# Modulation vectors of two transformer blocks: multiplying two row chunks of weights in one step instead of one

## The chip, the cores and the metric

The kernel runs on one core of a Trainium2 chip. The metric is the device time of one execution in microseconds (us); lower is better. Everything below concerns that one core, its engines and its DMA queues: PE (the matrix engine), DVE, ACT, POOL and SP, the last of which issues nearly all transfers.

## What is computed

Two blocks stand one behind the other in the same launch. The first takes 512 tokens of width 1024 through four layers (gated linear attention, a spatial gating unit, forgetting attention, gated linear attention again). The second takes them through two layers with a feed-forward part each; its first layer mixes a gated delta rule with latent attention, its second neighbourhood attention with grouped attention, and both also see 256 context tokens. Each layer is modulated by vectors that depend on the condition alone:

```python
def first_block(x, c, ...):
    cond = jax.nn.silu(c)
    for i in range(DEPTH):
        mod = (cond @ w_mod[i] + b_mod[i])[:, None, :]
        shift, scale, gate = jnp.split(mod, 3, axis=-1)
        h = rms_norm(x, norm_pre_g[i]) * (1.0 + scale) + shift
        ...
        x = x + gate * rms_norm(o, norm_post_g[i])
```

The second block does the same with six vectors for each layer and two conditions (one for the tokens, one for the context). So there are 4 x 3 + 2 x 6 = 24 vectors of 1024 numbers, each a product of a condition with a 1024 x 1024 matrix of fp32 weights, that is 4 MB to be read for each vector. The change touches only how 22 of them are made; the first two are made in a setup that it leaves alone.

## The kernel before, in words

The program is written as Python generators. A main generator walks through the layers; each of its yields marks a small piece of work (some tens of PE instructions). Two queues of background generators run beside it: "m" makes the modulation vectors and, near the end of it, a table of neighbourhood biases in DRAM (`nab`); "c" does the context tokens. `drain` (L416) steps each queue by a rate per yield of the main generator: 0.6 steps of queue "m" (`MRATE`). `step` (L399) adds up what is owed and takes whole steps. In the last column chunk of an output projection `proj_tok` also takes `MB` = 2 steps of queue "m" behind each row tile (L316 to L322). `need` (L411) takes steps until a vector that is wanted now is finished.

One vector is one run of `mods` (L373). Its weights go in eight row chunks of 128 x 1024 fp32 (512 KB). A chunk is loaded by SP (L382) into a tile of tag `wm`, of which there are two buffers (`WM` = 2), and multiplied by four matmuls of PE (L386). These stand in four column groups of one PSUM bank (tile `mods.pa`, 32 columns of the condition's padded tile as stationary and 256 moving columns each); an fp32 matmul is two passes, so a chunk is eight instructions on PE. The generator yields after each chunk: a step loads chunk k and multiplies chunk k - 1. After the last, DVE copies the bank to SBUF (L390) and SP stores the vector to a scratch tensor in DRAM (L392). That is eleven steps for a vector. `mod_cols` (L425) later loads two vectors of the scratch and their bias (tiles `mra`, `mrb`), DVE adds them (L432), and PE turns the sum into columns. `na_bias` (L1931) writes the table `nab` by 4 stores of a constant (L1940), 15 transfers for the border columns (L1947) and 8 for the inner ones (L1952), with yields between.

The generators set only the order in which the program is written. A scheduler then places each instruction on its engine by estimated readiness, so that chunks of one vector can be drawn together or apart. Within an engine the order is then fixed; an instruction that waits holds up all behind it. All loads are issued by SP, in turn: weight pieces of the projections (L279, tiles that end in `wr`, which ACT and POOL split into `wh` and `wl`), chunks `wm`, and small loads. Products of the main work read `wh` and `wl`: L307 to L309 for tokens as stationary or moving side, L351 to L353 for the others; the part of a tile's name ahead of the dot is the stage (`out` output projection, `sgu` gating unit, `gdng` delta rule, `mlap` latent attention's projections, `pre` norms).

Of the kernel before, what the change touches and what calls it, by code (L numbers as in the profile page):

```python
# [10 lines left out]
F32 = mybir.dt.float32  # L11
# [10 lines left out]
D = 1024  # L22
# [26 lines left out]
class Residual:  # L49
# [8 lines left out]
    def load(self):  # L58
        nc = self.core.nc
        self.tiles = [self.core.t("t4", (128, D)) for _ in range(self.nt)]  # L60
        for i, tl in enumerate(self.tiles):
            nc.sync.dma_start(tl, self.src[i * 128:(i + 1) * 128])
# [14 lines left out]
class Core:  # L77
# [295 lines left out]
    def mods(self, scr, cname, W, ncond, v):  # L373

        nc = self.nc
        pad = self.cond[cname]
        ps = self.psA()
        ws = []
        for k in range(8 + WM - 1):
            if k < 8:  # L380
                ws.append(self.wp.tile([128, D], F32, name=self.nm("wm"), tag="wm", bufs=WM))
                nc.sync.dma_start(ws[k], W[k * 128:(k + 1) * 128, v * D:(v + 1) * D])  # L382
            j = k - WM + 1
            if j >= 0:
                for g in range(4):
                    nc.tensor.matmul(ps[g * 32:(g + 1) * 32, :256], pad[:, j, :], ws[j][:, g * 256:(g + 1) * 256],  # L386
                                     start=(j == 0), stop=(j == 7))
            yield
        sb = self.t("t1", [128, 256])
        nc.vector.tensor_copy(sb, ps[:, :256])  # L390
        for i in range(ncond):
            nc.sync.dma_start(scr[i, v * D:(v + 1) * D].rearrange("(g n) -> g n", n=256), sb[i:128:32, :])  # L392
        yield
# [1656 lines left out]
    def ffn_layer(self, H, x, nt, mods, ic, i, nxt, dst=None):  # L2050
        A = self.A
        self.need(("b", i, 3))
        gg = self.gate_row(mods, ic, A["b_mod_2"][i], 5, A["g_post_ffn_2"][i])
        return (yield from self.phase("ffn", self.ffn(H, nt, i, x, gg, nxt, dst)))
# [59 lines left out]
    def even_out(self, x, nt, mods, ic, s, nxt):  # L2114
        A = self.A
        self.need(("b", 0, 1))
        gg = self.gate_row(mods, ic, A["b_mod_2"][0], 2, A["g_post_mix_2"][0])
        ffn = lambda: self.norm_before(x, nt, mods, ic, "ffn", 0)
        H = yield from self.phase("out", self.outproj(s["O"], nt, A["w_out_even_2"][0], 8, x, gg, ffn))
        if nt == 4:  # L2120
            self.context_rate(12)
        return (yield from self.ffn_layer(H, x, nt, mods, ic, 0, nxt))
# [76 lines left out]
WM, WSZ = 2, 512  # L2199
# [9 lines left out]
BANKS, ROLES = {"pp": 4, "pa": 4}, {}  # L2209
LO = {'': 'p', 'pre': 'ppd', 'c': 'ddp', 'cgdnp': 'd', 'cmlap': 'd', 'gla': 'ppd', 'oddq': 'pdd', 'coddkv': 'pd', 'gdnp': 'ppd', 'oddkv': 'pdd', 'out': 'ddp', 'cout': 'pd', 'mlap': 'ppd', 'fox': 'pdd', 'cmla': 'd'}  # L2210
PREA = (3,)
MRATE, MB = 0.6, 2
ADV = 1
PRI = 100
LEAD = (1, 1, 1, 1, 2)
# [66 lines left out]
```

## Time and profile before

| | us |
|---|---|
| runs | 3272.90, 3277.65, 3279.38 |
| median | 3277.65 |
| profiled execution, its own time | 3278.63 |
| its span, first to last instruction | 3276.8 |
| its mean granted PE clock | 0.975 |

The profiled execution lies 1.8 us outside its span and 1.0 us above the median of the runs. Busy times in the profile are sums over instructions; a matmul's end is modelled and overlaps the start of the next, so the cost of one in a chain is read from the starts of its neighbours. A wait in brackets, such as [1.62 <-DMA mods.wm<-in_w_mod_dram], is time in which the engine had nothing to run, and what ended it. A granted clock of 1.00 is 2.4 GHz, of 0.50 it is 1.2 GHz.

### The profile page before, as it was taken

How to read it: one execution, taken by the hardware profiler on the slowest of the kernel's cores; microseconds unless marked ns; L12 is line 12 of the kernel's file. 1: busy time of each engine (PE TensorE's matmuls, PEld its weight loads, DVE VectorE, ACT ScalarE, POOL GpSimd, SP SyncE). 2: the span in 40 equal slices, each digit the busy share in tenths (PEclk: the TensorE clock that was granted, in tenths of full speed). 3: DMA queues.
4: the chain of work that ended last, by engine and by line, in shares of the span. 5: the costliest groups of instructions: out<-in, count | busy, mean ns of one | idle time of the engine just before them, and what ended most of it. 6: DMA issues, size and time to landing. Idle time of an engine off the chain costs nothing.

```text
span 3276.8 us, 63046 instructions
## 1 busy us (share of the span) xinstructions
PE 3100.1 (95%) x24399; PEld 2687.7 (82%) x24399; DVE 1691.3 (52%) x3578; ACT 1460.2 (45%) x3205; POOL 1308.6 (40%) x1320
## 2 busy tenths in 40 slices
PE   6999999999999999988989999899999989999998
PEld 4878889778877778777877889899899867889898
DVE  2745564454555564666888667641113468641212
ACT  3434544454544533345545544453324457643323
POOL 2544454232212345344543123554445341254445
PEclk7999999999999999989999999899999999999999
DMA  7355645753436524444564334443333330143332
GB/s 238 91 157 168 210 139 162 246 162 118 135 120 186 184 80 136 129 140 141 166 164 133 102 94 138 140 136 94 97 120 111 109 84 2 41 131 96 96 121 87
DMA packets 487155, 426.36 MB, mean 130 GB/s; under 512 B 108038, under 2 KB 441065, under 8 KB 486857
## 3 DMA queue, kind: packets, MB, share of 16 engines
q1 hardware_dynamic: 486857, 422.35, 43.0%
q8 instruction: 192, 3.15, 0.4%
q14 instruction: 106, 0.87, 0.1%
HBM read 383.66 MB, written 38.03 MB: 129 GB/s over the span
## 4 chain that ended last, share of the span: by engine, by line
PE 74%; DVE 11%; DMA 5%; ACT 4%; issue 3%; POOL 2%; SPq 1%; DVEq 0%; POOLq 0%; ACTq 0%
PE ffn.pp L352 6%; PE ffn.pp L351 6%; PE ffn.pp L353 6%; PE ffn.pp L308 3%; PE ffn.pp L307 3%; PE ffn.pp L309 3%; PE mods.pa L386 3%; PE out.pp L307 2%; PE out.pp L309 2%; PE out.pp L308 2%; DMA mods.wm<-in_w_mod_dram 2%; PE fox.pp L308 1%; PE fox.pp L309 1%; PE fox.pp L307 1%; PE sgu.pp L307 1%
## 5 line engine op out<-in xcount | busy, mean ns | idle before, releaser
L257 POOL TENSOR_TENSOR ffn.wl<-ffn.wr,ffn.wh 128x512 fp32r<-128x512 f32 x258 | 333.6, 1294 | 355.2 <-ACT ffn.wh L256 355.2
L256 ACT ACTIVATE ffn.wh<-ffn.wr 128x512 fp32r<-128x512 f32 x258 | 162.5, 631 | 355.2 <-PE ffn.pp L353 144.3
L351 PE MATMUL ffn.pp<-pre.t,ffn.wh 128*128 128x512 f32 x672 | 261.5, 389 | 0.0
L352 PE MATMUL ffn.pp<-pre.t,ffn.wl 128*128 128x512 f32 x672 | 261.5, 389 | 0.0
L353 PE MATMUL ffn.pp<-pre.t,ffn.wh 128*128 128x512 f32 x672 | 261.4, 389 | 0.0
L308 PE MATMUL ffn.pp<-ffn.wl,ffn.t 128*128 128x256 f32 x656 | 185.3, 283 | 0.0
L309 PE MATMUL ffn.pp<-ffn.wh,ffn.t 128*128 128x256 f32 x656 | 184.9, 283 | 0.0
L307 PE MATMUL ffn.pp<-ffn.wh,ffn.t 128*128 128x256 f32 x656 | 184.7, 283 | 0.0
L591 DVE SCALAR_TENSOR_TENSOR ffn.t<-ffn.t,ffn.pp 128x512 f32<-128x512 f32 (+1 forms) x66 | 39.4, 597 | 252.1 <-ACT ffn.t L590 252.0
L257 POOL TENSOR_TENSOR gla.wl<-gla.wr,gla.wh 128x512 fp32r<-128x512 f32 x66 | 87.0, 1319 | 163.2 <-ACT gla.wh L256 153.6
L307 PE MATMUL gla.pp<-gla.wh,pre.t 128*128 128x256 f32 x512 | 150.0, 293 | 0.7 <-ACT gla.t L644 0.4
L309 PE MATMUL gla.pp<-gla.wh,pre.t 128*128 128x256 f32 x512 | 149.1, 292 | 0.9 <-DVE pre.t L257 0.9
L308 PE MATMUL gla.pp<-gla.wl,pre.t 128*128 128x256 f32 x512 | 149.1, 291 | 0.0
L353 PEld LDWEIGHTS ffn.pp<-pre.t,ffn.wh 128*128 128x128 f32 x672 | 126.1, 188 | 26.2
L351 PEld LDWEIGHTS ffn.pp<-pre.t,ffn.wh 128*128 128x128 f32 x672 | 126.2, 188 | 26.1
L352 PEld LDWEIGHTS ffn.pp<-pre.t,ffn.wl 128*128 128x128 f32 x672 | 126.2, 188 | 25.9
L257 POOL TENSOR_TENSOR ffn.cwl<-ffn.cwr,ffn.cwh 128x512 fp32r<-128x512 f32 x44 | 60.8, 1382 | 211.9 <-ACT ffn.cwh L256 172.7
L386 PE MATMUL mods.pa<-mods.wm,cond_c 128*32 128x256 f32 x1408 | 122.5, 403 | 16.0 <-DMA mods.wm<-in_w_mod_dram 15.9
L1133 DVE SCALAR_TENSOR_TENSOR ffn.t<-ffn.t,ffn.pp 128x512 f32<-128x512 f32 (+1 forms) x66 | 39.4, 597 | 176.3 <-PE ffn.pp L353 175.7
L256 ACT ACTIVATE ffn.cwh<-ffn.cwr 128x512 fp32r<-128x512 f32 x132 | 82.9, 632 | 102.2 <-PE ffn.pp L353 42.0
L308 PEld LDWEIGHTS ffn.pp<-ffn.wl,ffn.t 128*128 128x128 f32 x656 | 125.9, 192 | 0.2
L307 PEld LDWEIGHTS ffn.pp<-ffn.wh,ffn.t 128*128 128x128 f32 x656 | 125.6, 192 | 0.2
(815 smaller groups left out, 10808.3 us busy)
## 6 DMA issues: line engine op xcount, KB each, us to landing
mods.wm<-in_w_mod_dram SPq DMA_DIRECT2D x176, 512.0 KB
gla.wr<-in_gla_w_in_dram SPq DMA_DIRECT2D x96, 256.0 KB
ffn.wr<-in_w_ffn_gate_dram SPq DMA_DIRECT2D x88, 256.0 KB
ffn.wr<-in_w_ffn_up_dram SPq DMA_DIRECT2D x88, 256.0 KB
ffn.wr<-in_w_ffn_down_dram SPq DMA_DIRECT2D x88, 256.0 KB
fox.wr<-in_fox_w_in_dram SPq DMA_DIRECT2D x64, 256.0 KB
sgu.wr<-in_sgu_w_in_dram SPq DMA_DIRECT2D x48, 256.0 KB
out.res_x<-out.t SPq DMA_DIRECT2D x24, 512.0 KB
```

The source lines that it names most:

```text
L256: nc.scalar.activation(hi, src, AF.Copy)
L257: (lo_eng or nc.vector).tensor_tensor(lo, src, hi.bitcast(F32), op=ALU.subtract)
L307: nc.tensor.matmul(o, H.hi(kk, s), w[0][:, k], start=(kk == 0 and first), stop=False)
L308: nc.tensor.matmul(o, H.hi(kk, s), w[1][:, k], start=False, stop=False)
L309: nc.tensor.matmul(o, H.lo(kk, s), w[0][:, k], start=False, stop=(kk == K - 1 and last))
L351: nc.tensor.matmul(o, wh[:, k], H.hi(kk), start=(kk == 0), stop=False)
L352: nc.tensor.matmul(o, wl[:, k], H.hi(kk), start=False, stop=False)
L353: nc.tensor.matmul(o, wh[:, k], H.lo(kk), start=False, stop=(kk == K - 1))
L386: nc.tensor.matmul(ps[g * 32:(g + 1) * 32, :256], pad[:, j, :], ws[j][:, g * 256:(g + 1) * 256], start=(j == 0), stop=(j == 7))
L591: nc.vector.scalar_tensor_tensor(dst, dst, 1.0, z, ALU.add, ALU.mult)
L1133: nc.vector.scalar_tensor_tensor(f, sg, 0.5, o[1], ALU.mult, ALU.mult)
```

## The change

A step now deals with two chunks. The first step loads chunks 0 and 1; each of the next four multiplies the two chunks that are there and, but for the last, loads the next two. The copy to SBUF and the store follow in the last multiplying step. A vector takes six steps instead of eleven. The buffers stay two. The rate of queue "m" goes from 0.6 to 0.34 steps per yield of the main generator, which is 0.0545 vectors before and 0.0567 now; the steps behind each of the four row tiles of an output projection's last chunk go from 2 to 1, which is 8/11 of a vector before and 4/6 now. The bias table's steps come from the same queue at the same rates, and are as many as before.

```diff
         ps = self.psA()
-        ws = []
-        for k in range(8 + WM - 1):
-            if k < 8:
-                ws.append(self.wp.tile([128, D], F32, name=self.nm("wm"), tag="wm", bufs=WM))
-                nc.sync.dma_start(ws[k], W[k * 128:(k + 1) * 128, v * D:(v + 1) * D])
-            j = k - WM + 1
-            if j >= 0:
+
+        def load(k0):
+            ws = [self.wp.tile([128, D], F32, name=self.nm("wm"), tag="wm", bufs=WM) for _ in range(WM)]
+            for i, w in enumerate(ws):
+                nc.sync.dma_start(w, W[(k0 + i) * 128:(k0 + i + 1) * 128, v * D:(v + 1) * D])
+            return ws
+
+
+        nxt = load(0)
+        yield
+        for k0 in range(0, 8, WM):
+            ws = nxt
+            for i, w in enumerate(ws):
+                j = k0 + i
                 for g in range(4):
-                    nc.tensor.matmul(ps[g * 32:(g + 1) * 32, :256], pad[:, j, :], ws[j][:, g * 256:(g + 1) * 256],
+                    nc.tensor.matmul(ps[g * 32:(g + 1) * 32, :256], pad[:, j, :], w[:, g * 256:(g + 1) * 256],
                                      start=(j == 0), stop=(j == 7))
-            yield
+            if k0 + WM < 8:
+                nxt = load(k0 + WM)
+                yield
...
-MRATE, MB = 0.6, 2
+MRATE, MB = 0.34, 1
```

No instruction is added or left out; what changes is the order. In the changed program line numbers below the matmul are 9 higher (the matmul itself is L393 there). On PE the matmuls of the 176 chunks stand in 171 unbroken runs before and in 138 now. On SP 50 of the chunks' loads are followed directly by another before, 77 now, and 92 by a weight piece before, 74 now. Three places follow.

**First place, PE, in the stage of the gating unit's projections** (`mods.pa_915` before and `mods.pa_901` now are the bank of one vector; `wm` with a number is a chunk). Before:

```order
L308 MATMUL sgu.pp_911_4668<-sgu.wl928_4771,pre.t4_676_3351 128x256
L309 MATMUL sgu.pp_911_4668<-sgu.wh927_4770,pre.t4_680_3355 128x256
L386 MATMUL mods.pa_915_4699<-mods.wm916_4700,cond_c_2_435 32x256 x4
L351 MATMUL gdnp.pp_894_4577<-pre.t4_763_3773,gdnp.cwh931_4806 128x256
L352 MATMUL gdnp.pp_894_4577<-pre.t4_763_3773,gdnp.cwl932_4807 128x256
```

Now:

```order
L308 MATMUL sgu.pp_914_4673<-sgu.wl923_4725,pre.t4_677_3358 128x256
L309 MATMUL sgu.pp_914_4673<-sgu.wh922_4724,pre.t4_681_3362 128x256
L393 MATMUL mods.pa_901_4626<-mods.wm902_4627,cond_c_2_432 32x256 x4
L393 MATMUL mods.pa_901_4626<-mods.wm903_4628,cond_c_2_432 32x256 x4
L351 MATMUL gdnp.pp_894_4577<-pre.t4_763_3774,gdnp.cwh927_4766 128x256
L352 MATMUL gdnp.pp_894_4577<-pre.t4_763_3774,gdnp.cwl928_4767 128x256
```

The vector's second chunk, which stood 37 rows behind the first, now follows it at once: two runs have become one.

**Second place, PE, the vector of bank `mods.pa_729`, in the gating unit's projections** (`ident` as an input marks a transpose, `.mra` the modulation columns). Before, the vector's first two chunks stand 35 main products (L307 to L309, all of `sgu.pp_743`) ahead of these rows, which end with the third chunk:

```order
L309 MATMUL sgu.pp_743_3679<-sgu.wh784_3874,pre.t4_681_3356 128x256
L796 MATMUL sgu.pa_740_3671<-ident_72,sgu.t2_739_3669 128x128 x4
L434 MATMUL .pa_755_3755<-ident_72,.mra_753_3750 128x16
L307 MATMUL sgu.pp_743_3679<-sgu.wh784_3874,pre.t4_677_3352 128x256
L308 MATMUL sgu.pp_743_3679<-sgu.wl785_3875,pre.t4_677_3352 128x256
L494 MATMUL pre.pa_766_3776<-ident_72,pre.t4_761_3769 128x128 x4
L386 MATMUL mods.pa_729_3651<-mods.wm750_3740,cond_c_86 32x256 x4
```

Now:

```order
L309 MATMUL sgu.pp_743_3675<-sgu.wh784_3870,pre.t4_683_3364 128x256
L805 MATMUL sgu.pa_740_3667<-ident_72,sgu.t2_739_3665 128x128 x4
L393 MATMUL mods.pa_729_3651<-mods.wm730_3652,cond_c_86 32x256 x4
L393 MATMUL mods.pa_729_3651<-mods.wm731_3653,cond_c_86 32x256 x4
L443 MATMUL .pa_756_3757<-ident_72,.mra_754_3752 128x16
L503 MATMUL pre.pa_767_3778<-ident_72,pre.t4_762_3771 128x128 x4
L503 MATMUL pre.pa_769_3790<-ident_72,pre.t4_762_3771 128x128 x4
L393 MATMUL mods.pa_729_3651<-mods.wm747_3714,cond_c_86 32x256 x4
L307 MATMUL mlap.pp_788_3910<-mlap.cwh790_3913,pre.t4_763_3774 128x160
```

The first two chunks have moved behind those products. Between them and the third chunk, which goes into a buffer that they free, three rows of transposes are left of what was 41 rows, 38 of them products.

**Third place, SP and DVE, at the transition from the first block's last output projection to the second block** (`nab` is the bias table, `out.mra` the load of two finished vectors for the second block's first norm). SP before:

```order
L279 DMA mlap.wr3500_17422<-in_w_in_even_2_dram 128x2x256
L1940 DMA nab_16710<-mods.t4_3350_16711 128x960 x4
L279 DMA mlap.wr3506_17470<-in_w_in_even_2_dram 128x2x256
L279 DMA mlap.wr3512_17518<-in_w_in_even_2_dram 128x2x256
L392 DMA mod_b1_220<-mods.t1_3329_16622 4x256 x2
L1952 DMA nab_16710<-in_na_rpb_2_dram 15x49x16 x4
L1947 DMA nab_16710<-in_na_rpb_2_dram 8x15x16 x11
L1566 DMA gdng.t2_3366_16820<-gdn_sg_ctx_4571 128x256
L1947 DMA nab_16710<-in_na_rpb_2_dram 8x15x16 x4
L1952 DMA nab_16710<-in_na_rpb_2_dram 15x49x16 x4
L430 DMA out.mra_3519_17558<-mod_b0_219 16x128
```

SP now:

```order
L279 DMA mlap.wr3500_17419<-in_w_in_even_2_dram 128x2x256
L1949 DMA nab_16537<-mods.t4_3321_16538 128x960 x4
L279 DMA mlap.wr3506_17467<-in_w_in_even_2_dram 128x2x256
L1961 DMA nab_16537<-in_na_rpb_2_dram 15x49x16 x2
L279 DMA mlap.wr3512_17515<-in_w_in_even_2_dram 128x2x256
L1961 DMA nab_16537<-in_na_rpb_2_dram 15x49x16 x4
L1956 DMA nab_16537<-in_na_rpb_2_dram 8x15x16 x11
L1575 DMA gdng.t2_3366_16820<-gdn_sg_ctx_4571 128x256
L1956 DMA nab_16537<-in_na_rpb_2_dram 8x15x16 x4
L439 DMA out.mra_3519_17556<-mod_b0_219 16x128
```

Behind the last `mlap.wr` load, four of the eight inner-column transfers and the store of `mod_b1` (which has gone some ten rows up) no longer stand ahead of the load of `out.mra`. DVE's add of that load, before:

```order
L554 TENSOR_TENSOR out.t4_3271_16226<-out.pp_3340_16691,.t4_3239_16057 128x256
L585 SCALAR_TENSOR_TENSOR out.t4_3307_16479<-out.t4_3271_16226,out.rr_3357_16774,out.t4_3307_16479 128x512 x2
L1553 SCALAR_TENSOR_TENSOR Sfin_489<-gdng.t4_3155_15617,gdnglb_ctx_4525,gdng.pa_3364_16800 64x64 x4
L1561 TENSOR_TENSOR gdng.t2_3323_16563<-gdng.t2_3323_16563,gdng.pa_3364_16800 64x2x128
L1553 SCALAR_TENSOR_TENSOR Sfin_489<-gdng.t4_3154_15616,gdnglb_ctx_4525,gdng.pa_3365_16810 64x64 x4
L1561 TENSOR_TENSOR gdng.t2_3323_16563<-gdng.t2_3323_16563,gdng.pa_3365_16810 64x2x128
L432 TENSOR_TENSOR out.mra_3519_17558<-out.mra_3519_17558,out.mrb_3520_17559 16x128
```

DVE now:

```order
L441 TENSOR_TENSOR out.mra_3519_17556<-out.mra_3519_17556,out.mrb_3520_17557 16x128
L563 TENSOR_TENSOR out.t4_3275_16252<-out.pp_3341_16702,.t4_3242_16071 128x256
L594 SCALAR_TENSOR_TENSOR out.t4_3308_16487<-out.t4_3275_16252,out.rr_3357_16778,out.t4_3308_16487 128x512 x2
L1562 SCALAR_TENSOR_TENSOR Sfin_486<-gdng.t4_3159_15626,gdnglb_ctx_4525,gdng.pa_3364_16800 64x64 x4
L1570 TENSOR_TENSOR gdng.t2_3325_16574<-gdng.t2_3325_16574,gdng.pa_3364_16800 64x2x128
L1562 SCALAR_TENSOR_TENSOR Sfin_486<-gdng.t4_3158_15625,gdnglb_ctx_4525,gdng.pa_3365_16810 64x64 x4
L1570 TENSOR_TENSOR gdng.t2_3325_16574<-gdng.t2_3325_16574,gdng.pa_3365_16810 64x2x128
```

The add has moved ahead of the six rows that it stood behind.

## Rows read from the trace of the kernel before

**Rows 1.** The page: busy time by engine; chain that ended last, by engine and line.

```profile
PE 3100.1 (95%) x24399; PEld 2687.7 (82%) x24399; DVE 1691.3 (52%) x3578; ACT 1460.2 (45%) x3205; POOL 1308.6 (40%) x1320
...
PE 74%; DVE 11%; DMA 5%; ACT 4%; issue 3%; POOL 2%; SPq 1%; DVEq 0%; POOLq 0%; ACTq 0%
PE ffn.pp L352 6%; PE ffn.pp L351 6%; PE ffn.pp L353 6%; PE ffn.pp L308 3%; PE ffn.pp L307 3%; PE ffn.pp L309 3%; PE mods.pa L386 3%; PE out.pp L307 2%; PE out.pp L309 2%; PE out.pp L308 2%; DMA mods.wm<-in_w_mod_dram 2%; PE fox.pp L308 1%; PE fox.pp L309 1%; PE fox.pp L307 1%; PE sgu.pp L307 1%
```

**Rows 2.** PE's waits for chunks (total, times, longest): whole, 590 to 700, 905 to 930.

```profile
PE mods.pa L386 <- DMA mods.wm<-in_w_mod_dram: 15.9, 17, 2.2
PE mods.pa L386 <- DMA mods.wm<-in_w_mod_dram: 6.5, 5, 2.2
PE mods.pa L386 <- DMA mods.wm<-in_w_mod_dram: 2.2, 2, 1.6
```

**Rows 3.** Waits of SP's own queue for chunks' matmuls, whole span, same columns.

```profile
SPq L382 <- PE mods.pa L386: 215.7, 121, 15.1
```

**Rows 4.** Timeline, PE, 302.8 to 304: start, duration, form, count [idle]; one chunk.

```profile
302.88 0.28 PE L308 MATMUL out.pp<-out.wl,gla.t 128*128 128x256 f32 x1
303.00 0.28 PE L309 MATMUL out.pp<-out.wh,gla.t 128*128 128x256 f32 x1
303.20 0.64 PE L386 MATMUL mods.pa<-mods.wm,cond_c 128*32 128x256 f32 x8
303.77 0.38 PE L307 MATMUL out.pp<-out.wh,gla.t 128*128 128x256 f32 x1
```

**Rows 5.** Timeline, PE, 309.3 to 310.8: two chunks in one run.

```profile
309.38 0.28 PE L309 MATMUL out.pp<-out.wh,gla.t 128*128 128x256 f32 x1
309.59 1.07 PE L386 MATMUL mods.pa<-mods.wm,cond_c 128*32 128x256 f32 x16
310.59 0.39 PE L307 MATMUL out.pp<-out.wh,gla.t 128*128 128x256 f32 x1
```

**Rows 6.** Timeline, SP, 911 to 915: two chunks' loads issued one behind the other.

```profile
912.54 1.18 SPq L382 DMA_DIRECT2D mods.wm<-in_w_mod_dram  x2
```

**Rows 7.** Timeline, PE, 916 to 918: the same two chunks' matmuls.

```profile
916.70 0.64 PE L386 MATMUL mods.pa<-mods.wm,cond_c 128*32 128x256 f32 x8 [1.62 <-DMA mods.wm<-in_w_mod_dram]
917.93 0.65 PE L386 MATMUL mods.pa<-mods.wm,cond_c 128*32 128x256 f32 x4 [0.59 <-DMA mods.wm<-in_w_mod_dram]
```

**Rows 8.** Timeline, PE, 352 to 364, the second place: first pair and third chunk.

```profile
352.23 1.07 PE L386 MATMUL mods.pa<-mods.wm,cond_c 128*32 128x256 f32 x16
...
360.87 0.64 PE L386 MATMUL mods.pa<-mods.wm,cond_c 128*32 128x256 f32 x8
```

**Rows 9.** Timeline, SP, 352.9 to 354: the loads that follow the first pair.

```profile
352.93 1.02 SPq L382 DMA_DIRECT2D mods.wm<-in_w_mod_dram  x2
```

**Rows 10.** Timeline, SP, 1415 to 1445, the third place.

```profile
1416.02 5.12 SPq L279 DMA_DIRECT2D mlap.wr<-in_w_in_even_dram  x2
1421.24 1.03 SPq L392 DMA_DIRECT2D mod_b<-mods.t  x2
...
1439.48 3.39 SPq L1952 DMA_DIRECT2D nab<-in_na_rpb_dram  x4
1442.97 1.06 SPq L430 DMA_DIRECT2D out.mra<-mod_b  x1
```

**Rows 11.** Timeline, DVE, 1438 to 1451, the third place.

```profile
1438.86 1.42 DVE L585 SCALAR_TENSOR_TENSOR out.t<-out.t,out.rr,out.t 128x512 f32<-128x512 f32 x2 [0.37 <-POOL out.rr L532]
1440.31 0.85 DVE L1553 SCALAR_TENSOR_TENSOR Sfin<-gdng.t,gdnglb_ctx,gdng.pa 64x64 f32<-64x64 f32 x4
1441.17 0.42 DVE L1561 TENSOR_TENSOR gdng.t<-gdng.t,gdng.pa 64x256 f32<-64x256 f32 x1
...
1449.62 0.28 DVE L432 TENSOR_TENSOR out.mra<-out.mra,out.mrb 16x128 f32<-16x128 f32 x1 [6.71 <-DMA out.mra<-mod_b]
```

**Rows 12.** Timeline, PE, 1445 to 1456: the wait that ends there.

```profile
1453.88 0.66 PE L1047 MATMUL gdng.pa<-ident,gdng.t 128*128 128x128 f32 x2 [9.00 <-DVE gdng.t L1573]
```

**Rows 13.** Busy time, 918 to 928: PE, PEld, DVE, ACT, POOL, clock, DMA share, GB/s.

```profile
918.00:928.00 10.00, 10.00 (x44) 5.28 (x44) 4.21 (x17) 2.96 (x11) 0.00 (x0) 0.51 0.44 122
```

## The prediction

> **What bounds the kernel now.** I read the page first: PE is busy 3100.1 us and makes 74% of the chain that ended last, DVE 11% and transfers 5%; the chunk matmuls are 3% of that chain and their loads 2% [rows 1]. So PE bounds the kernel nearly everywhere, and a change of order is worth what it saves PE in work or in idle time. Next come the waits: PE sits idle for chunks 15.9 us in 17 places, 6.5 us of it between 590 and 700 and 2.2 us between 905 and 930 [rows 2]. SP stands at the head of its queue for chunks' matmuls far longer, 215.7 us in 121 places [rows 3]; that costs nothing by itself, but it shows that a chunk's load is issued when the matmuls that free its buffer end. Then the timeline: what a run of chunk matmuls costs PE beyond its columns [rows 4, 5], how long a load takes from issue to use [rows 6, 7], and the places where the order of the rows changes [rows 8 to 12].
>
> **Fewer runs on PE.** One chunk between two main products holds them 303.77 - 303.00 = 0.77 us apart; without it they are 303.00 - 302.88 = 0.12 us apart, so the chunk costs 0.65 us [rows 4]. Two chunks in one run cost 310.59 - 309.38 - 0.12 = 1.09 us [rows 5]. Two single runs are 1.30, so one run merged into another saves 0.21 us; the same difference from unrounded times is 0.226. The order has 171 runs before and 138 now: 33 x 0.226 = **-7.5 us** of PE time. If only PE's share of the chain counts, it is 0.74 x 7.5 = -5.6, which is my weaker end for this term while PE stays the bound.
>
> **Waits for chunks.** Both programs keep two buffers, and chunk k is loaded when chunk k - 2 has been multiplied; a pair in a step does not load earlier. What decides is how much PE work the order leaves between the two. I counted it, each row of the order at its line's mean cost in the trace: 16 of these stretches are under 4 us before, 13 now; the median shrinks from 9.4 to 8.5 us. From 590 to 700 and from 905 to 930 the rows around the chunks are the same in both, so 8.7 us in 7 places stay [rows 2]. The other ten waits, 15.9 - 8.7 = 7.2 us, lie where the order changes. Most of their stretches grow, by 0.5 to 2.5 us; each growth counted up to the wait that it meets gives -5.5, with ends of -7.2 (all go) and 0.
>
> New waits come at two kinds of place. At the second place the first pair and the third chunk were 360.87 - 352.23 = 8.64 us apart [rows 8], and the load that the first chunk freed went out at 352.93 [rows 9]. Now one chunk's matmuls and three rows of transposes are left between, 1.9 us by the count. The earliest of two loads issued together was used 916.70 - 912.54 = 4.16 us after the issue [rows 6, 7]. So PE waits 4.16 - 1.9 = **+2.3 us** there, with the latent attention's first product behind it. The other kind is the second load of a pair, used 917.93 - 912.54 = 5.39 us after the first's issue, 1.2 us after the first chunk, with a wait of its own of 0.59 [rows 6, 7]. In nine places the order now leaves a second chunk a stretch that short or hardly longer. The ends are 0 and 9 x 1.2 = 10.8; I take half of the places at 0.59, **+2.7**, since that wait is the nearest row and half of the stretches exceed 5.39. Together the waits come to -5.5 + 2.3 + 2.7 = **-0.5 us**.
>
> **SP behind the second load.** SP now stops for both chunks' matmuls before it goes on to weight pieces (77 loads are followed by another chunk's, 50 before). Where the pair is one run on PE, that delays the pieces by a chunk's half microsecond, and the pieces already there cover it, POOL and ACT being busy 40 and 45% [rows 1]. Where the scheduler drew the pair apart, SP is held up to the 15.1 us that it is held now at the worst [rows 3]. I price it at 0; its bad end is the second rival.
>
> **The first norm of the second block.** DVE sat idle 6.71 us for the load of `out.mra` [rows 11], issued at 1442.97 [rows 10], and behind that PE waited 9.00 us for DVE [rows 12]. The store (1.03) and four table transfers (3.39) no longer stand between the last wait of SP for a weight buffer (the 5.12 at 1416.02) and that load [rows 10], so it goes out 4.4 us earlier. But the add has moved ahead of six rows of DVE's: 0.42 (a row of that size), 1.42 and two pairs of 0.85 and 0.42, that is 4.4 us [rows 11], which were done while DVE waited and now stand behind the wait. **0**, with ends -4.4 (the load is there when DVE comes) and +4.4 (the load lands no earlier, since the transfers that it follows fill the queues).
>
> **The number of steps and rates.** Vectors advance at 0.0567 for 0.0545 per yield and 4/6 for 8/11 in the projections' last chunks, so they finish at nearly the same places; what that moves is in the order and counted above. 0.
>
> **Sum.** -7.5 - 0.5 + 0 = -8.0 against the profiled execution's 3278.63: **3270.6 us**. That execution stands 1.0 above the median of 3277.65, so this is -0.22% of the median. About 0.2%, 6.6 us, is what a measurement of this kernel can tell from no change: faster means below 3271.1, slower above 3284.2. The forecast's own range is 3266 to 3275: down by 2.7 (no second load is late) and 1.7 (the last of the ten waits go too), up by 1.9 (the weaker end of the runs) and 2.7 (twice the second loads).
>
> **A rule against the row on the clock.** After the waits at 916.70 and 917.93 PE's granted clock was 0.51, the 1.2 GHz level, over 10 us in which PE was busy throughout [rows 13]; such a stretch holds about 5 us more than the same work at 2.4 GHz. The waits that I add have no such stretch in my sum, since most chunk waits are shorter than these two together and sit between long runs of products. The Trainium skill, "TensorE: Matmul & The Clock Gate", section "HAM oscillation — how this bites in real kernels", says that a gap in which TensorE waits for a transfer throws it back to half clock, again at every such gap; the trace agrees for this one [rows 13]. By that rule each new wait of the second place's kind would cost such a stretch, and the sum would be 3275.6 instead of 3270.6.
>
> **Rivals.** *Further down.* All ten movable waits go, no second load is late, and the load for the norm wins its whole 4.4 us: -7.5 - 7.2 + 2.3 - 4.4 = -16.8, 3261.8. For it: fewer short stretches, SP's 4.4 us are read from rows. Against it: DVE's reordering takes the last term back unless the load lands by the time that DVE arrives, which now is earlier as well.
>
> *No change.* Two ways lead there. PE's saved time comes back as waits on ACT, POOL or SP, because weight pieces issued behind a held second load are late; or the change does not do what it says, since the scheduler pulls pairs apart: all pairs together would leave 88 runs, and the order keeps 138. The second is counted already. The first gives 3278.6 - 0.5 = 3278, within 3275 to 3281. For it: transfers busy 5% of the chain, SP held 215.7 us [rows 1, 3]. Against it: 74% of the chain is PE.
>
> *Slower.* The two loads of a pair go out together, and the second comes 1.2 us behind the first; where a step multiplies both, PE stops for the second. Before, 126 of the 176 loads had no other chunk's right behind them. With all nine places at 1.2, the second place's 2.3, none of the old waits gone, and one more stretch at 0.51 behind them: -7.5 + 2.3 + 10.8 + 5 = +10.6, 3289.2. It decides once second loads take longer than their stretch of 5.4 us. For it: the second of two loads does wait in the trace [rows 7]. Against it: half of the stretches are longer. The Trainium skill, "DMA: Bandwidth & Descriptors", section "Queues, rings and completion order", speaks for this rival: each transfer engine consumes one issuer's descriptors in ring order, so that the second load can't be served beside the first. The 1.2 us between the two uses [rows 7] agrees with it.
>
> **How the numbers follow.** Forecast 0.40, further down 0.20, no change 0.22, slower 0.18. Of the forecast's range 3266 to 3275 some 0.57 lies below 3271.1. Faster is 0.40 x 0.57 + 0.20 = 0.43; the same 0.40 x 0.43 + 0.20 of no change = 0.37; slower 0.18 + 0.02 = 0.20. The range of 3260 to 3286 takes in the forecast, no change, most of the way down, and the lower part of slower; it leaves out some 0.14 above and 0.05 below.
>
> **What would show it.** Chunk matmuls in 138 runs, their mean cost to neighbours down, PE's total wait for chunks between 13 and 18 us, a new wait of about 2.3 us for a chunk near 360 us, `out.mra` issued some 4 us earlier and PE's wait for DVE there still near 9. The prediction is wrong if PE's waits for chunks exceed 20 us, if weight pieces (waits of PE on POOL or ACT) gain more than 5 us, or if new stretches at 0.5 of the clock appear.

## The result, and the profile after

The changed kernel takes 3298.02 us in the median of six runs (3288.96 to 3310.32), the kernel before 3278.52 on the same chip (3272.90 to 3284.18). The ratio is 1.0063, interval 1.0045 to 1.0080: slower by 0.63%, where the prediction had -0.22% and a range that ended at 3286.0. The profiled execution of the changed kernel took 3307.14, in the upper half of its runs; its span is 3305.1, 28.3 us more than before. The page's first line:

```profile
PE 3117.5 (94%) x24399; PEld 2713.3 (82%) x24399; DVE 1685.8 (51%) x3578; ACT 1460.5 (44%) x3205; POOL 1311.0 (40%) x1320
```

Against [rows 1] PE has the same instructions, and yet 3117.5 - 3100.1 = 17.4 us more busy time; it is idle for 3305.1 - 3117.5 = 187.6 us instead of 3276.8 - 3100.1 = 176.7, 10.9 more. The two make the 28.3. The work is the same, in 138 runs of chunks instead of 171, so the additional busy time goes with the clock as far as the profile tells: the mean granted clock is 0.969 where it was 0.975 (the view of cores), so PE stood at 1.2 GHz for 2 x (1 - 0.969) x 3305 = 205 us after 164.

```profile
core 0: 3305.1 us, clock 0.969
```

PE's waits in the changed kernel, from the view of waits (engine, line, what it waited for: total us, times, longest), some of PE's longest entries, then SP's own queue:

```profile
PE pre.pa L503 <- DVE pre.t L532: 24.1, 8, 7.3
PE mods.pa L393 <- DMA mods.wm<-in_w_mod_dram: 13.7, 13, 3.1
...
PE glah.pa L732 <- POOL glah.t L725: 11.0, 13, 1.3
PE gdng.pa L1056 <- DVE gdng.t L1582: 7.8, 3, 5.7
...
PE glah.pa L787 <- DVE glah.t L783: 4.8, 2, 4.5
```

```profile
SPq L382 <- PE mods.pa L393: 196.9, 101, 17.9
```

The counterparts of the lines for `pre.t`, POOL and `gdng` in the kernel before:

```profile
PE pre.pa L494 <- DVE pre.t L523: 20.1, 8, 7.3
...
PE gdng.pa L1047 <- DVE gdng.t L1573: 10.5, 3, 9.0
PE glah.pa L723 <- POOL glah.t L716: 9.0, 16, 1.2
```

The waits for chunks, which the prediction was about, are 13.7 us after 15.9 [rows 2], and SP's waits for them 196.9 after 215.7 [rows 3]. What grew are waits for other engines: summed over all of PE's entries, those for DVE go from 79.2 to 88.1 us, those for ACT from 31.7 to 35.5, those for POOL from 18.9 to 22.0. A place that shows it well is the start of a group of forgetting attention near 1000 us. The timeline of PE before, the rows with chunks alone:

```profile
995.60 0.64 PE L386 MATMUL mods.pa<-mods.wm,cond_c 128*32 128x256 f32 x8
...
996.78 0.64 PE L386 MATMUL mods.pa<-mods.wm,cond_c 128*32 128x256 f32 x8 [0.23 <-DMA mods.wm<-in_w_mod_dram]
...
999.84 0.64 PE L386 MATMUL mods.pa<-mods.wm,cond_c 128*32 128x256 f32 x8 [0.81 <-DMA mods.wm<-in_w_mod_dram]
```

The same place after, the rows with a chunk or a wait:

```profile
1006.22 1.07 PE L393 MATMUL mods.pa<-mods.wm,cond_c 128*32 128x256 f32 x16
...
1009.75 0.50 PE L1033 MATMUL fox.pp<-fox.t,fox.t 128*128 128x256 f32 x2 [1.95 <-ACT fox.t L1014]
...
1011.06 0.57 PE L1034 MATMUL fox.pp<-fox.t,fox.t 66*128 66x256 f32 x1 [0.45 <-DVE fox.t L1015]
...
1015.14 0.48 PE L898 MATMUL fox.pa<-ident,fox.at 128*128 128x128 f32 x1 [1.94 <-ACT fox.at L873]
```

Busy time there (PE, PEld, DVE, ACT, POOL, clock, DMA share, GB/s), before and then after:

```profile
995.00:1005.00 10.00, 8.60 (x64) 4.76 (x63) 8.84 (x28) 8.14 (x24) 1.27 (x1) 1.00 0.66 208
```

```profile
1011.00:1021.00 10.00, 8.00 (x30) 4.98 (x31) 9.35 (x38) 4.04 (x16) 0.00 (x0) 0.50 0.11 36
```

Before, three single chunks stood one by one between short products whose inputs ACT was still making. They were **cover**: PE multiplied them while it would have waited. After, the last two chunks of the vector go through in one run ahead of the first of those products. Then PE waits 1.95 for ACT, and at 1011 its clock falls to 1.2 GHz for ten microseconds. The rows behind lie 4.4 us later than the rows ahead, each taken against its counterpart before.

The second place, after (compare [rows 8]); the timeline of PE and the busy time behind it:

```profile
372.08 1.07 PE L393 MATMUL mods.pa<-mods.wm,cond_c 128*32 128x256 f32 x16
...
375.12 1.09 PE L503 MATMUL pre.pa<-ident,pre.t 128*128 128x128 f32 x8 [1.81 <-DVE pre.t L532]
376.87 1.08 PE L393 MATMUL mods.pa<-mods.wm,cond_c 128*32 128x256 f32 x8 [0.66 <-DMA mods.wm<-in_w_mod_dram]
```

```profile
376.00:383.00 7.00, 6.16 (x35) 4.84 (x37) 5.01 (x13) 5.17 (x10) 0.70 (x2) 0.52 0.68 234
```

I had expected a wait of 2.3 us for the chunk's load. It is 0.66, because PE first waits 1.81 for DVE, whose result the transposes between need; before, main products stood there. (The two waits together, 2.47, are close to what I had expected for the load.) Then again the clock is at the lower level.

The third place, after: SP's load of `out.mra`, DVE's add, PE's wait (compare [rows 10 to 12]).

```profile
1469.63 0.39 SPq L439 DMA_DIRECT2D out.mra<-mod_b  x1
```

```profile
1471.34 0.28 DVE L441 TENSOR_TENSOR out.mra<-out.mra,out.mrb 16x128 f32<-16x128 f32 x1 [4.25 <-DMA out.mra<-mod_b]
```

```profile
1479.67 0.66 PE L1056 MATMUL gdng.pa<-ident,gdng.t 128*128 128x128 f32 x2 [5.74 <-DVE gdng.t L1582]
```

The load is used 1471.34 - 1469.63 = 1.7 us after its issue, 6.65 before, and PE's wait is 5.74 instead of 9.00. This place gains.

To see where time goes I compared the start of every PE instruction other than the chunks with that of its counterpart before (22991 of them) and took the median difference by stretch, for the two profiles above and for a second profile of each of the two programs (the last experiment below):

| stretch of the kernel before, us | first profiles | second profiles |
|---|---|---|
| 100 to 150 | 1.3 | 3.1 |
| 250 to 300 | 11.2 | 6.0 |
| 350 to 400 | 16.2 | 10.1 |
| 600 to 650 | 15.8 | 7.0 |
| 950 to 1000 | 10.9 | 8.7 |
| 1000 to 1050 | 16.0 | 14.7 |
| 1100 to 1150 | 22.5 | 21.2 |
| 1400 to 1450 | 29.1 | 29.9 |
| 1450 to 1500 | 25.5 | 25.2 |
| 3200 to the end | 28.4 | 22.7 |

Both columns lose at the same places: 4 to 5 us at the second place (350), 5 to 6 at the attention's start (1000), 6.5 to 7.5 near 1100, and over 5 ahead of 1400. Both win about 4 at the third place (1450). Of the 11.2 us of the first 300 us only 6.0 come again, and that needs an explanation of its own.

### The profile page after: what moved, and what is told of

The parts are those of the page before. It is cut to its first block, busy times and chain, and to the rows that moved or that the text cites. A ratio compares the mean times of both kernels' runs of the same rounds, so it can differ in the third digit from the quotient of the medians.

```text
span 3305.1 us, 63046 instructions
## 1 busy us (share of the span) xinstructions
PE 3117.5 (94%) x24399; PEld 2713.3 (82%) x24399; DVE 1685.8 (51%) x3578; ACT 1460.5 (44%) x3205; POOL 1311.0 (40%) x1320
## 4 chain that ended last, share of the span: by engine, by line
PE 42%; DVE 5%; ACT 1%; POOL 1%; issue 1%; DMA 0%; DVEq 0%; POOLq 0%; SPq 0%; ACTq 0%
PE ffn.pp L352 6%; PE ffn.pp L351 6%; PE ffn.pp L353 5%; PE ffn.pp L308 3%; PE ffn.pp L307 3%; PE ffn.pp L309 3%; PE odda.pa L1089 1%; PE odda.pa L898 1%; PE mla.pp L1705 1%; PE mla.pa L1089 1%; PE out.pp L309 1%; PE out.pp L307 1%; PE out.pp L308 1%; PE gdng.pa L1553 1%; PE mla.pa L898 1%
## 5 line engine op out<-in xcount | busy, mean ns | idle before, releaser
L309 PE MATMUL ffn.pp<-ffn.wh,ffn.t 128*128 128x256 f32 x656 | 184.9, 283 | 0.0
L307 PE MATMUL ffn.pp<-ffn.wh,ffn.t 128*128 128x256 f32 x656 | 184.7, 283 | 0.0
L307 PE MATMUL gla.pp<-gla.wh,pre.t 128*128 128x256 f32 x512 | 151.7, 297 | 6.0 <-DVE gla.t L654 2.7
L309 PE MATMUL gla.pp<-gla.wh,pre.t 128*128 128x256 f32 x512 | 152.7, 299 | 1.7 <-DVE pre.t L257 1.7
L393 PE MATMUL mods.pa<-mods.wm,cond_c 128*32 128x256 f32 x1408 | 118.1, 409 | 14.2 <-DMA mods.wm<-in_w_mod_dram 13.7
L307 PEld LDWEIGHTS ffn.pp<-ffn.wh,ffn.t 128*128 128x128 f32 x656 | 125.6, 192 | 0.2
```

Of the source, the lines that this page charges most:

```text
L307: nc.tensor.matmul(o, H.hi(kk, s), w[0][:, k], start=(kk == 0 and first), stop=False)
L309: nc.tensor.matmul(o, H.lo(kk, s), w[0][:, k], start=False, stop=(kk == K - 1 and last))
```

## The experiments

All ratios are to runs of the kernel before on the same chip.

| kernel | median, us | ratio | interval |
|---|---|---|---|
| the change | 3298.02 | 1.0063 | 1.0045 to 1.0080 |
| pair_old_pace | 3312.26 | 1.0092 | 1.0075 to 1.0109 |
| pair_033 | 3294.73 | 1.0038 | 1.0025 to 1.0051 |
| pair_036 | 3286.84 | 1.0017 | 1.0004 to 1.0030 |
| pair_037 | 3293.59 | 1.0044 | 1.0030 to 1.0058 |
| pair_038 | 3305.64 | 1.0088 | 1.0070 to 1.0106 |
| pair_load_single_mult | 3307.49 | 1.0082 | 1.0062 to 1.0101 |
| single_new_pace | 3300.65 | 1.0058 | 1.0043 to 1.0073 |
| single_059 | 3306.10 | 1.0081 | 1.0056 to 1.0105 |
| single_061 | 3306.97 | 1.0074 | 1.0051 to 1.0097 |
| single_062 | 3301.80 | 1.0063 | 1.0043 to 1.0083 |
| one_vector_pairs | 3288.69 | 1.0026 | 1.0017 to 1.0035 |
| one_vector_singles | 3291.52 | 1.0036 | 1.0026 to 1.0047 |
| pairs_where_busy | 3280.87 | 1.0012 | 1.0003 to 1.0020 |
| pairs_where_waiting | 3288.70 | 1.0038 | 1.0026 to 1.0051 |
| three_vectors_pairs | 3281.84 | 1.0008 | 0.9995 to 1.0020 |

**Pairs, pace, or loads.** The change does two things: two chunks a step, and a new pace of the queue. Four kernels take them apart.

```diff
 pair_old_pace (the changed kernel)
-MRATE, MB = 0.34, 1
+MRATE, MB = 0.6 * 6 / 11, 12 / 11
 single_new_pace (the kernel before)
-MRATE, MB = 0.6, 2
+MRATE, MB = 0.34 * 11 / 6, 11 / 6
 pair_load_single_mult (the changed kernel)
             for i, w in enumerate(ws):
+                if i:
+                    yield
                 j = k0 + i
...
-MRATE, MB = 0.34, 1
+MRATE, MB = 0.34 * 10 / 6, 10 / 6
 single_061 (the kernel before)
-MRATE, MB = 0.6, 2
+MRATE, MB = 0.61, 2
```

> The pairs are kept, but queue m goes at the pace of before in vectors (0.6/11 of a vector for each yield, 8/11 behind an output projection's tiles). If multiplying two chunks in a run is what costs the time (fewer single chunks to stand between the short products of other stages, so PE idles and its clock falls): still slower than before by 12 to 25 us, with about 200 us at the lower clock level as in the changed kernel. If the pace costs it: within 6 us of before. If any other order than the one before costs it: slower by anything from 5 to 30 us.

> The step of before (one chunk), at the pace of the changed kernel in vectors (0.34/6 of a vector for each yield, 4/6 behind an output projection's tiles). If the pairs cost the time: within 6 us of before, mean clock about 0.975. If the pace costs it: slower by 12 to 25 us, clock about 0.970. If any other order costs it: slower by 5 to 30 us.

> Chunks are loaded in pairs as in the changed kernel, but multiplied one in a step (ten steps for a vector, at the same pace in vectors as the changed kernel). If the runs of two on PE cost the time: within 6 us of before. If the paired loads on SP cost it: slower by 12 to 25 us, as the changed kernel. If any other order costs it: slower by 5 to 30 us.

> The kernel before with a rate of 0.61 instead of 0.60 steps for each yield and nothing else; no part of the change is in it. If pairs, pace or paired loads cost the time: within 4 us of before, since a vector moves by less than 2%. If any other order than the one before costs it: slower by 5 to 30 us, with the mean clock below 0.975.

None is within 6 us of before. Neither the pairs, nor the pace, nor the paired loads is the cause alone: a rate of 0.61 instead of 0.60, with nothing of the change in it, costs 0.74%. The third theory, that leaving the order before costs, is the one that fits all four, though `pair_old_pace`, 32.0 us slower, lies 2 us beyond the range that I gave for it.

**More paces.** Two more of single chunks, four more of pairs, each with one number changed:

```diff
 single_059, single_062 (the kernel before)
-MRATE, MB = 0.6, 2
+MRATE, MB = 0.59, 2
...
+MRATE, MB = 0.62, 2
 pair_033, pair_036, pair_037, pair_038 (the changed kernel)
-MRATE, MB = 0.34, 1
+MRATE, MB = 0.33, 1
...
+MRATE, MB = 0.36, 1
...
+MRATE, MB = 0.37, 1
...
+MRATE, MB = 0.38, 1
```

> The kernel before with 0.59 instead of 0.60 steps for each yield; nothing of the change in it. If the order before is simply one that suits the other work well, and any other loses that: slower than before by 10 to 30 us, with 110 to 130 us of PE's work at the lower clock level (91 in the profile of before). If a faster background is what costs (0.61 was slower): within 6 us of before.

> The kernel before with 0.62 instead of 0.60 steps for each yield; nothing of the change in it. If any other order than the one before loses: slower by 10 to 30 us. If the pairs are what costs, kernels of single chunks without the order of before should lie well below those of pairs: at most 10 us above before.

> The changed kernel with 0.33 instead of 0.34 steps for each yield. If the pairs cost time of their own, beyond the loss of the old order: 3305 to 3320 us, above the kernels of single chunks at other paces. If only the order counts: anywhere between 3285 and 3315, as these.

> The changed kernel with 0.36 instead of 0.34 steps for each yield. The same two cases as for 0.33: 3305 to 3320 us if pairs cost time of their own, anywhere between 3285 and 3315 if only the order counts; in both, the sum of PE's idle time and half of its work at the lower clock level should explain the time to within 15 us, as it does in the five profiles so far.

> The changed kernel with 0.37 instead of 0.34 steps for each yield. If a faster background is the better pace for pairs (0.36 was the best so far): 3275 to 3290 us. If times scatter with the order and have no trend in the pace: anywhere between 3285 and 3315.

> The changed kernel with 0.38 instead of 0.34 steps for each yield. If a faster background is the better pace for pairs: 3275 to 3290 us. If times scatter with the order and have no trend in the pace: anywhere between 3285 and 3315.

Single chunks at four other paces lie at 1.0058 to 1.0081, pairs at six paces at 1.0017 to 1.0092, with means of 1.0069 and 1.0057. Pairs are not worse than single chunks that have lost the order before, and no trend in the pace can be seen: 0.36 is best, 0.38 nearly worst. So 0.63% is an ordinary price here for drawing the background's chunks anew. None of these paces is under the kernel before. The other half of the expectation for 0.36 failed: what a profile's span leaves after PE's idle time and half of PE's busy time at the lower clock runs from 3030 to 3059 us over the ten programs up to here, a spread of 29 where I had written 15, so these two sums are not the whole account. What is missing shows when all 19 profiles of this case are sorted by their runs of chunks on PE: the eight with 138 to 148 runs leave 3030 to 3043 us, the eleven with 155 to 185 leave 3045 to 3059. So fewer runs do save PE work, by an estimate from the means of these two groups (3035 and 3051) some 16 us, about twice what I had counted. The price is paid elsewhere: PE is idle for 182.0 to 200.3 us in the profiles of pairs at six paces, 177.5 to 182.7 in those of single chunks at the four other paces, and 169.2 and 176.7 in the two of the kernel before.

**One vector.** Can a single lost cover be shown? The sixteenth vector is the one whose last chunks stand at 995 to 1000 us. `one_vector_pairs` makes it alone in pairs, in eleven steps as before, so that no other step moves; 99% of PE's other rows keep their order among themselves. `one_vector_singles` is the changed kernel with that vector alone in single chunks, which also changes the order behind it.

```diff
 one_vector_pairs (the kernel before)
+        self.made = getattr(self, "made", -1) + 1
+        if self.made == 15:
+            for k0 in range(0, 10, 2):
+                for j in range(max(k0 - 2, 0), k0):
+                    for g in range(4):
...
+                for k in range(k0, min(k0 + 2, 8)):
...
+                yield
+                if k0 < 8:
+                    yield
 one_vector_singles (the changed kernel)
+        if self.made == 15:
+            self.rate["m"] = MRATE * 11 / 6
+            for k in range(9):
...
+                yield
+            self.rate["m"] = MRATE
...
```

> The kernel before, with one vector alone (the sixteenth that queue m makes, whose last three chunks stand where PE would otherwise wait for ACT at the start of a forgetting-attention group, near 1000 us) multiplied in pairs, in as many steps as before. The order of the other rows stays as it is. If single chunks are cover for the waits of other stages: one or two new waits of PE of 1 to 2 us between 995 and 1005, a new stretch at the lower clock level of 7 to 14 us behind them, and the rows behind 1020 us later by 3 to 7 us than in the profile of before. If pairs as such cost nothing: rows behind 1020 us within 1 us of before.

> The changed kernel, with that one vector alone made in single chunks (its eleven steps at 11/6 of the rate). If single chunks are cover: the waits of 1.95 and 1.94 us and the lower clock between 1009 and 1021 us of the changed kernel shrink, and the rows behind go earlier by 2 to 6 us against those ahead. If not: that stretch stays as it is. The order behind it changes, so that the total may lie anywhere between 3285 and 3315.

One vector of 22 costs 0.26%, 8.5 us. The timeline of PE in `one_vector_pairs`, the pair and the first wait behind it, and the busy time from there:

```profile
985.08 1.07 PE L384 MATMUL mods.pa<-mods.wm,cond_c 128*32 128x256 f32 x16
...
988.72 0.79 PE L1037 MATMUL fox.pp<-fox.t,fox.t 128*128 128x256 f32 x2 [2.06 <-ACT fox.t L1018]
```

```profile
988.00:998.00 10.00, 9.28 (x43) 5.35 (x43) 5.58 (x21) 5.12 (x17) 0.81 (x1) 0.52 0.62 215
```

It is the picture of the changed kernel: the pair, a wait for ACT of 2.06 us that was not there, the clock at 0.52. The rows go from 9.75 us earlier than in the profile of before to 5.71 earlier, a loss of 4.0 at this one place, as the theory of cover expected. (The vector's last two chunks still stand singly there, behind the wait: the scheduler drew that pair apart.) A stretch of 10 us at the lower level stands at this place in all three profiles that have the pair (the changed kernel's two and this one) and in neither profile of the kernel before. The rest of the 8.5 comes elsewhere, where some other rows did move; that part is not settled. The other way round, the single chunks in the changed kernel take the 1.95 and the 1.94 away (0.9 and 1.1 are left), and the rows behind go some 2 us earlier. The whole goes from 1.0063 to 1.0036, but these intervals meet and the order behind the vector is another, so that this difference shows nothing by itself.

**Other vectors.** The edit of `one_vector_pairs` at other vectors:

```diff
 pairs_where_busy, pairs_where_waiting, three_vectors_pairs (one_vector_pairs)
-        if self.made == 15:
+        if self.made in (3, 6, 7, 8, 12, 16):
...
+        if self.made in (13, 17, 18, 20):
...
+        if self.made in (6, 7, 8):
```

> The kernel before, with six vectors multiplied in pairs, in as many steps as before: those whose chunks stand among long runs of main products, where PE does not wait (the fourth, seventh, eighth, ninth, thirteenth and seventeenth that queue m makes). PE's runs of chunks go from 171 to 155; the other rows keep their order but for some 3%. If single chunks cost only where they are cover: 16 x 0.226 = 3.6 us faster, ratio 0.998 to 1.000. If any displacement from the order before costs: slower by 0.2% or more.

> The same edit at four vectors whose chunks stand among short products of other stages, with waits near them (the fourteenth, eighteenth, nineteenth and twenty-first). If single chunks are cover there: slower by 3 to 15 us (0.1 to 0.5%), with new waits or new stretches at the lower clock level near 850, 1100 or 1330 us. If only the number of runs counted (171 to 167): 1 us faster.

> The kernel before, with three vectors multiplied in pairs, in as many steps as before (the seventh, eighth and ninth that queue m makes, between 430 and 620 us, among long runs of main products). PE's runs of chunks go from 171 to 165. If a run less saves 0.226 us where no wait is near: rows behind 620 us are 1.4 us earlier against those ahead of 430 (3 at most, as in the profile of the six vectors), and the whole lies 1 to 3 us under before, a ratio of 0.999 to 1.000. If any displacement costs: slower by 0.1% or more.

Four vectors among short products cost 0.38%; six among long runs of main products cost 0.12%, although they save four times as many runs (16 for 4). The totals go the way that cover would have them go, but the profile of the four vectors does not show cover. From 750 to 1300 us, past three of the four, its rows stay between 4.5 and 7.4 us ahead of the first profile of before, and no wait of 1 us comes up at them. The loss, 11 us, lies between 1300 and 1420, in two parts. At the fourth vector PE waits for the chunks themselves; two waits and the busy time behind them (PE, PEld, DVE, ACT, POOL, clock, DMA share, GB/s):

```profile
1325.52 0.64 PE L384 MATMUL mods.pa<-mods.wm,cond_c 128*32 128x256 f32 x8 [2.24 <-DMA mods.wm<-in_w_mod_dram]
...
1333.80 0.91 PE L384 MATMUL mods.pa<-mods.wm,cond_c 128*32 128x256 f32 x8 [2.64 <-DMA mods.wm<-in_w_mod_dram]
```

```profile
1334.00:1344.00 10.00, 10.00 (x110) 9.18 (x103) 2.73 (x10) 2.79 (x6) 0.00 (x0) 0.50 0.21 66
```

In the first profile of before the longest wait for a chunk there is 1.64. So some 6 us go by loads that come too late for pairs, nearer to the slower rival than to cover. The other 5 go near 1404, where the vector at work is made one chunk a step, as before:

```profile
1403.98 0.44 PE L791 MATMUL glah.pa<-ident,glah.t 128*128 128x128 f32 x2 [2.93 <-DVE glah.t L787]
```

That is main work that moved with the order. So cover is shown at the vector near 1000 us, and not at these four.

The six are not 3.6 us faster. In their profile the rows between 400 and 650 us do go 3.2 us earlier against the second profile of before (6.25 late to 3.03), while 8 us are lost ahead of that, between 250 and 400, around a vector that I had taken for harmless; how much of these is chance of the clock the one profile doesn't tell. The three vectors between 430 and 620 gain 2.0 us there against the first profile of before (2.09 early to 4.06), but the two profiles of before, with the same order, differ by 2.5 us over the same stretch, so that 6 x 0.226 = 1.4 can't be read from it. The whole is no faster (0.9995 to 1.0020).

**The same program twice.** The kernel after and the kernel before, unchanged, each profiled once more.

> The changed kernel itself, profiled once more. If the clock falls by chance at a given wait: the stretches at the lower level near 154, 212 and 274 us of the first profile (27 us together) are not all there again, and the rows behind 290 us lie 5 to 15 us earlier with the same order of instructions. If they belong to the order: the same three stretches, rows within 2 us.

> The kernel before, profiled once more. If the clock falls by chance: the long stretch near 733 us (13.7) or those ahead of 80 us may be gone, others may be new, the time within 10 us of the first profile. The waits of PE themselves, which belong to the order, should repeat to within 3 us in total (168 us of idle time in the first profile).

They took 3292.28 and 3269.43 us, 14.9 and 9.2 less than in their first profiles, with the same order of instructions. Such a spread is there on a single chip too: 20 executions of the kernel before on the chip of these two took from 3269.34 to 3283.71 us, with a mean clock from 0.973 to 0.979. The view of cores, the kernel before and then the kernel after:

```profile
core 0: 3267.6 us, clock 0.980
```

```profile
core 0: 3290.3 us, clock 0.969
```

The clearest row is in the kernel before; PE's timeline near 733 us and its busy time (PE, clock, DMA share, GB/s), first profile, then second:

```profile
733.02 0.33 PE L889 MATMUL fox.pa<-ident,fox.at 128*128 128x128 f32 x1 [1.07 <-ACT fox.at L864]
```

```profile
730.00:750.00 20.00, 18.93 (x108) 0.66 0.51 152
```

```profile
732.74 0.33 PE L889 MATMUL fox.pa<-ident,fox.at 128*128 128x128 f32 x1 [1.07 <-ACT fox.at L864]
```

```profile
730.00:750.00 20.00, 18.74 (x165) 1.00 0.55 174
```

The same wait of 1.07 us was followed by the lower clock once and not the other time, and the rows behind it differ by 5 to 6 us. In the kernel after it is the gated linear attention's waits for POOL; busy time at 140 to 165 us in its two profiles:

```profile
140.00:165.00 25.00, 22.30 (x156) 0.80 0.23 66
```

```profile
140.00:165.00 25.00, 22.23 (x192) 1.00 0.28 85
```

Two of the three stretches of the first profile were gone (154 us) or shorter (212), the third was there again, and the rows behind 290 us lay 8 us earlier. So at a given short wait the clock falls in one execution and not in another; what decides, the runs do not show. The waits belong to the order, but the idle time of PE held less well than expected, 169.2 us in the second profile of before (its span of 3267.6 less the 3098.4 in which PE is busy) after 176.7. In the second profile of the kernel after, two more places of the table show their wait:

```profile
1105.95 1.94 PE L503 MATMUL pre.pa<-ident,pre.t 128*128 128x128 f32 x8 [2.80 <-DVE pre.t L532]
```

```profile
1419.80 0.69 PE L787 MATMUL glah.pa<-ident,glah.t 128*128 128x128 f32 x2 [4.83 <-DVE glah.t L783]
```

Neither has a counterpart of more than 1.5 us in the second profile of before. Both are waits of main work for DVE, as at the second place. Summed over all of PE's entries, the waits for DVE are 87.0 us in the second profile of the kernel after and 76.1 in that of the kernel before, so this part of the loss comes again.

## Why the prediction was wrong

**Fewer runs on PE (-7.5): the mechanism held, and its size was if anything too small.** The order's 138 runs are in the trace. Sorted by runs, the 19 profiles put the saving of PE work at some 16 us. It did not make the kernel faster, since waits and the clock took more than that back.

**Waits for chunks (-0.5): the total held, its parts did not.** 15.9 became 13.7, and 14.2 became 13.1 in the second profiles, where 15.4 was forecast. The 2.3 us at the second place are 0.66, since PE was already held there by DVE, and the second loads left no mark in the total. That the parts cancelled is luck. The slower rival, which rested on the second loads, had the right side by the wrong mechanism for this kernel.

**The first norm of the second block (0): its good end came.** PE's wait fell by 3.3 us (by 4.3, from 6.9 to 2.6, in the second profiles), the rows gained 3.6 and 4.7. The load of `out.mra` was used 1.7 us after its issue, 6.65 before, so DVE's reordering did not take it back.

**The step that failed is "The number of steps and rates", where I wrote that what the pace moves "is in the order and counted above. 0."** I had counted the waits that PE has *for* chunks, and taken the rows that no term spoke of as unchanged in price. The runs put 19 to 27 us in the place of that 0: each of four other paces of single chunks, with no pair in them, costs 0.58 to 0.81%. In the two pairs of profiles PE's waits for DVE, ACT and POOL grow by 15.8 and 15.9 us, and its time at 1.2 GHz by 41 and 73. The kernel before sits at one good point of a rough surface, as far as the ten other paces tell, and a change that moves every chunk by a few rows should have been priced from there: most likely slower, by some tens of microseconds, whatever it saves by itself. Which rows make that point good, beyond the vector at 1000 us, the runs do not settle.

**A second part of that step: the waits that chunks fill.** At the vector near 1000 us single chunks stood between short products whose inputs ACT was still making; merged, they uncover waits of about 2 us, with the lower clock behind them, and 4 to 5 us are lost. The rows to see it were there: three chunks singly between 995.6 and 1000 us, in a stretch where the clock stayed at 1.00. How much of the rest is lost cover and how much is main work that moved is not shown; at the second place and near 1105 and 1420 it is main work that waits.

**On the clock** I weighed the rule of the Trainium skill ("TensorE: Matmul & The Clock Gate", section "HAM oscillation — how this bites in real kernels") against the row and left it out of the sum. PE's time at 1.2 GHz grew from 164 to 205 us, and from 131 (2 x 0.020 x 3267.6) to 204 in the second profiles; new stretches at half clock were among my own signs of being wrong. So the rule, that a gap in which TensorE waits for a transfer throws it back to half clock, pointed the right way, but the sum with it, 3275.6, still lay below the time before, because I had applied it to waits for chunks alone. That section of the Trainium skill tells it of a kernel with longer waits for transfers; here the clock fell behind waits of 1 to 2 us for ACT and DVE as well. That it happens at every such gap, this case does not bear out: the wait of 1.07 us at 733 was followed by it in one profile of two.

## What to carry to other kernels

Work that is ready early can be worth more between short, dependent instructions than in one block, even if each piece costs a switch: before merging it, look at what each piece now stands in front of, and price the wait that it covers. Where a scheduler redraws the whole order after a small change of pace, try a few neutral changes of pace first; what they cost (here 0.58 to 0.81%) is what any reordering has to beat. And profile the same program twice before explaining a difference by its places.

## What the runs showed that I had not expected

The granted clock after a short wait is not a property of the program alone. With the same order of instructions, one profile of the kernel before stood at 0.66 between 730 and 750 us and another at 1.00, behind the same wait of 1.07 us. The rows behind that place differ by 5 to 6 us. Two executions of one program, with such stretches here and there, lay 9.2 and 14.9 us apart, which is more than the 8.0 us that I had forecast.
